# The output projection of a hybrid decoder block: the last four token blocks by seven half products a pair, the attention rows of its weights converted ahead, and three factor chains in place of seven

## The chip, the cores and the metric

The kernel runs on one core of one Trainium2 chip. The metric is the device time of one execution in microseconds (us), the median of several runs. The engines are TensorE (PE in the profile; PEld is its loading of the stationary operand), VectorE (DVE), ScalarE (ACT), GpSimd (POOL), and SyncE (SP), whose queue here issues every DMA.

## What is computed

One decoder block on x (1024 tokens by 1024 columns, float32):

```python
h = rmsnorm(x, norm1_w)
proj = h @ w_in                      # 1024 x 4104, split into heads, gates and decays
o_sb  = rmsnorm(stick_breaking_attention(q, k, v), sb_norm_w)  * silu(sb_z)    # 8 heads of 64
o_gdn = rmsnorm(gated_delta(gq, gk, gv, decay, beta), gdn_norm_w) * silu(g_z)  # 4 heads of 128
mixed = concatenate([o_sb, o_gdn])   # 1024 x 1024
out = rmsnorm(x + mixed @ w_out, final_norm_w)
```

The change concerns the last two lines, and the factors 1/sqrt(mean square) that scale the attention's output, head by head and token by token.

## The kernel before

**How products are made.** A float32 product is three passes of a faster format, called float32r in the code: each operand is split into a high part (h: a copy rounded by ScalarE) and a low part (l: the operand less h), and `mm3` (line 533) adds h·h, h·l and l·h into a PSUM bank of 128 x 512. A product of 128 tokens by 512 columns over 1024 rows is 8 x 3 = 24 matmuls; over 512 rows, a half product here, it is 12.

**How the order is set.** The program is not written in its final order. `block` (line 439) starts generators, such as projections, attention, the delta rule, and the output's parts, and a planner (`Model`, lines 138 to 311) decides: it keeps a list of ready instructions for VectorE, ScalarE, GpSimd and SyncE, sorted by a priority (`ck.prio`, the names on line 35; a lower number goes first), with estimated costs and delays (`cost`, `HOPS`). `interleave` (line 409) picks the generator that may issue TensorE work. What comes out is a fixed order on each engine. At run time each engine, and the SyncE queue, takes its instructions in that order, and one that waits holds up all behind it. Because each recorded operation goes through one helper, almost all instructions carry line 329 in the profile; they are told apart by tile names.

**The end of the program.** The projections run as filler down to the eight gate blocks z0 to z7 (line 30), each in two halves (".0" is the lower 512 tokens). Each half ends in a VectorE multiplication by `rbc` (zt<-pp,rbc), a sigmoid and a GpSimd product; the gates go to DRAM (gate_s), except that of z7. Then:

- `factors` (line 1470): for the four pairs of attention heads j, and for j = 3 for each quarter p of the tokens by itself, the mean squares (ss_s in DRAM) are loaded into `sst`, VectorE takes the root in ten steps on `rst` and `ust`, and the result is stored (rs_s). That makes seven chains.
- `out_weights` (line 1502): the eight row blocks of w_out are loaded (wor), scaled by the norm weights and split into woh and wol. Rows 4 to 7 (delta) come early; rows 0 to 3 (attention) are split when the projections are over, since their tiles take the memory of the projections' operand x (xh, xl). Only then is `fnw`, the final norm's weight, loaded.
- `mixed_delta` (line 1531) and `mixed_attention` (line 1545): for a token block b of 128, the delta rule's output (mx) and its gates (gt), and the attention's output (oa), its factors (rb) and its gates (ga) are loaded. VectorE scales mx by rsg; GpSimd multiplies rb by the gates.
- `prepare` (line 1562): the delta half is transposed on TensorE (pz<-step,mx) and multiplied by the gates, the attention half is oa times rb (mf), and both are split into mh and ml, the low part by GpSimd.
- `product` (line 1594): for each block, 16 pairs of a 512-column half and a row block, each three matmuls: 48 a block. Blocks 0 and 1 take their delta halves (rows 4 to 7) first, because these are ready before the attention's. VectorE adds the residual (y), ScalarE sums squares, VectorE takes the root (`_rsqrt1`, tiles sy and ry), scales, and SyncE stores the block. The last block's upper half goes in two pieces of 256 columns, so that its end is short.

The few lines that carry the product before:

```python
for n, k in [(n, k) for n in range(len(parts)) for k in ks]:
    if k < 4 and b == 0:
        yield wts[k][2]
    hs = parts[n]
...
    mm3(pt, mh[:, k, :], ml[:, k, :], wts[k][0][:, hs], wts[k][1][:, hs], k == 4, k == 3)
```

Of the kernel before, what the change touches and what calls it, by code (L numbers as in the profile page):

```python
# [10 lines left out]
F32 = mybir.dt.float32  # L11
# [6 lines left out]
P = 128  # L18
T = 1024
# [15 lines left out]
OUT_WEIGHTS, DELTA, WEIGHTS, COMBINED, LATE, BANK, SPLIT, RSTD, WINDOW, OUTPUT, RESULT, DECAYS = -1, 0, 2, 3, 0.5, 5, 4, -0.5, 10, 12, 20, 25  # L35
# [358 lines left out]

class Stream:
# [43 lines left out]
def block(tc, xT_d, x_d, n1_d, wE_d, wC_d, conv_d, alog_d, dtb_d, mixw_d, wo_d, fnw_d, out_d):  # L439
# [4 lines left out]
    with ExitStack() as top:  # L444
# [31 lines left out]
        sst, rst, ust = [cst.tile([P, 16], F32, name=n) for n in ("sst", "rst", "ust")]  # L476
# [24 lines left out]
        px = open_pool("px", ctx=proj_ctx, side="right")  # L501
        xh = px.tile([P, NK, T], F32R, name="xh")
        xl = px.tile([P, NK, T], F32R, name="xl")
# [70 lines left out]
        for k in korder:  # L574
# [228 lines left out]
        def z_evac(i):  # L803
            n = (i + 4) % NK

            def evac(pt, half):
                hs = slice(half * 512, (half + 1) * 512)
                zt = pr.tile([P, 512], F32, tag="kt", bufs=2, name="zt")
# [479 lines left out]
        def gdn_chain(h, g):  # L1288
# [6 lines left out]
            for j in range(4):  # L1295
# [29 lines left out]
                def out(c=c, j=j, s_in=s_prev, vr=vr):  # L1325
# [4 lines left out]
                    oe = gi[0].tile([P, P], F32, tag="goe", name="goe")  # L1330
# [139 lines left out]
        def factors():  # L1470
            for j, p in [(0, 3), (1, 3), (2, 3)] + [(3, p) for p in range(4)]:
                yield from until(f"t{j}{p}")
                m = 16 if j < 3 else 4
                ss, rs, us = [t[:, 0:m] for t in (sst, rst, ust)]
                src, dst = [(d[j] if j < 3 else d[j, p]).rearrange("p h t -> (p h t)" if j < 3 else "h t -> (h t)").rearrange("(q f) -> q f", f=m) for d in (ss_s, rs_s)]
                yield S.dma_start(ss, src)
                _rsqrt(V, None, rs, ss, m, us)
                r = S.dma_start(dst, rs)
                for b in range(NB) if j < 3 else (2 * p, 2 * p + 1):
                    flags[f"c{j}{b}."] = r  # L1480
                yield


        wts = {}
        pools = {}

        def wo_raw(k):
            pool, tag, bufs = {4: (pools[0], "wor", 1), 5: (pools[0], "xr", 1), 6: (pools[0], "mh", 1), 7: (pools[0], "ml", 1),  # L1490
                               0: (at_, "v2a", 2), 1: (at_, "kh", 1), 2: (at_, "sg7", 1), 3: (at_, "v2a", 2)}[k]
            r = pool.tile([P, D], F32, tag=tag, bufs=bufs, name="wor")
            wts[k] = r
            return S.dma_start(r, wo_d[k * P:(k + 1) * P, :])

        def wo_split(k):
            w, pool = wts[k], pools[k < 4]
            wh, wl = [pool.tile([P, D], F32R, name=f"wo{n}{k}") for n in "hl"]
            A.activation(wh, w, AF.Copy, scale=mixw[:, k:k + 1])
            wts[k] = (wh, wl, V.scalar_tensor_tensor(wl, w, mixw[:, k:k + 1], wh.bitcast(F32), ALU.mult, ALU.subtract))  # L1500

        def out_weights():
            yield lambda: "g" in flags
            gdn_ctx.close()
            pools[0] = open_pool("f0", before=gd.ops() + gi[0].ops())
            flags["pool0"] = True
            raws = [wo_raw(k) for k in range(4, NK)]
            for k in range(4, NK):
                yield raws[k - 4]
                wo_split(k)  # L1510
            flags["wo"] = True
            yield lambda: f"s{SBH - 1}{NB - 1}" in flags
            for k in (0, 1):
                wo_raw(k)
            flags["late"] = True
            yield lambda: f"e{SBH - 1}{NB // 2 - 1}" in flags
            for k in (2, 3):
                wo_raw(k)
            yield lambda: "proj" in flags
            proj_ctx.close()  # L1520
            pools[1] = open_pool("f1", before=px.ops(), side="right")
            for k in range(4):
                ck.prio = LATE if k else OUT_WEIGHTS
                wo_split(k)
            fnw = wts["fnw"] = pools[1].tile([P, D], F32, name="fnw")
            S.dma_start(fnw, fnw_d.partition_broadcast(P))
            flags["fnw"] = True

        ready = {}

        def mixed_delta():
            for b in range(NB):
                yield lambda: "wo" in flags and "rsg" in flags and "z3" in flags and (b < 2 or "late" in flags and f"e{SBH - 1}{NB // 2 - 1}" in flags) and (b < 3 or "fnw" in flags and f"m{b - 3}" in flags)
                fi = pools[0]
                mx = fi.tile([P, 512], F32, **(dict(tag="wor") if b % 3 == 2 else dict(tag="mx", bufs=2, turn=True)), name="mx")
                gt = (at_.tile([P, 4, P], F32, tag="sg4", name="gt") if b % 3 == 2 else fi.tile([P, 4, P], F32, tag="gt", bufs=2, turn=True, name="gt"))
                S.dma_start(mx, og_s[b].rearrange("p h d -> p (h d)"))
                S.dma_start(gt, gate_s[4:8, :, b * P:(b + 1) * P].rearrange("k e t -> e k t"))
# [4 lines left out]
                flags[f"mx{b}1"] = r  # L1543

        def mixed_attention():
            for b in range(NB):
                bs = slice(b * P, (b + 1) * P)
                yield lambda: all(f"c{j}{b}." in flags for j in range(4)) and "z6" in flags and (b < 2 or f"l{b - 2}" in flags)
                oa, rb, ga = [pools[0].tile([P, n, P], F32, tag=t, bufs=2, turn=True, name=t) for t, n in (("oa", 4), ("rb", 4), ("ga", 3))]
                S.dma_start(oa, o_s[:, :, bs].rearrange("j r t -> r j t"))  # L1550
                for u in range(2):
                    S.dma_start(rb[64 * u:64 * u + 64], rs_s[:, b // 2, u, (b % 2) * P:(b % 2) * P + P].unsqueeze(0).to_broadcast([SBD, 4, P]))
                S.dma_start(ga, gate_s[0:3, :, bs].rearrange("k e t -> e k t"))
                G.tensor_tensor(rb[:, 0:3, :], rb[:, 0:3, :], ga, ALU.mult)
                yield lambda: ("z7" if b >= 4 else "z7.0") in flags
                ready["oa", b] = (oa, rb)
                flags[f"oa{b}0"] = G.tensor_tensor(rb[:, 3, :], rb[:, 3, :], gate7[b // 4][:, (b % 4) * P:(b % 4) * P + P], ALU.mult)

        def halves():
            return [(0, 1), (1, 1), (0, 0), (1, 0)] + [(b, g) for b in range(2, NB) for g in (1, 0)]  # L1560

        def prepare():
            for b, g in halves():
                bs = slice(b * P, (b + 1) * P)
                if g:
                    yield from until(f"mx{b}1")
                    mx, gt = ready["mx", b]
                    yield lambda: b == 0 or "late" in flags and (b < 2 or f"f{b - 2}" in flags)
                    pool = (pools[0], at_)[b % 2]
# [122 lines left out]
```

## Time and profile before

| | us |
|---|---|
| median of 3 runs | 665.47 (664.96 to 666.32) |
| the profiled execution | 666.25 |
| its span, first to last instruction | 664.5 |
| TensorE busy in the span | 647.4 |
| VectorE busy | 529.6 |
| ScalarE busy | 404.1 |
| GpSimd busy | 314.1 |
| mean granted TensorE clock | 0.995 |

The profile is one execution. The time of the profiled execution is 1.75 us longer than its span. In rows of a timeline the first number is the start from the span's beginning, the second the length, both in us; `out<-in` are tile names with their numbers left out, and the bracket at the end is the idle time before the instruction and what ended it. In group rows the count stands behind x, then busy us, mean ns of one, and the idle time before them. In rows of windows the engines follow as TensorE, weight loads, VectorE, ScalarE, GpSimd, then the granted clock, the DMA engines' share and GB/s.

### The profile page before, as it was taken

To read this page: it belongs to the slowest core of one execution; us is meant where nothing else is said; L and a number is where in the kernel's file an instruction comes from. 1 tells how busy PE (TensorE), PEld (TensorE's weight loads), DVE (VectorE), ACT (ScalarE), POOL (GpSimd) and SP (SyncE) were. 2 spreads that over 40 slices of the span, in tenths; PEclk is the share of its full clock that TensorE was granted. 3 is DMA by queue.
4 is the path that set the end of the run, shared out by engine and by line. 5 is a ranking of instruction groups with operands and counts; after the bars stand their busy time and mean duration, and the time that the engine had idled before them with its cause. 6 is when DMAs were issued, how large, how long until landed. Compare 5 with 4: busy or idle time off the path is not lost.

```text
span 664.5 us, 11883 instructions
## 1 busy us (share of the span) xinstructions
PE 647.4 (97%) x3950; PEld 550.8 (83%) x3950; DVE 529.6 (80%) x1122; ACT 404.1 (61%) x1028; POOL 314.1 (47%) x285
## 2 busy tenths in 40 slices
PE   8999999999999999999999999999999999899995
PEld 8998888888778888788888888888888888687884
DVE  6998789776998779887787889887878973779643
ACT  7975675544796758865868775577858642122121
POOL 0000212059952689536894238983354652632511
PEclk9999999999999999999999999999999999899999
DMA  8846852487061462217254226343165657567421
GB/s 314 324 159 206 280 192 95 161 259 236 24 187 45 143 232 70 61 48 239 73 171 119 69 62 203 115 128 120 24 208 184 224 163 223 142 220 203 149 78 63
DMA packets 81965, 103.22 MB, mean 155 GB/s; under 512 B 17808, under 2 KB 51696, under 8 KB 81904
## 3 DMA queue, kind: packets, MB, share of 16 engines
q1 hardware_dynamic: 81904, 102.47, 48.4%
q8 instruction: 31, 0.51, 0.3%
q14 instruction: 30, 0.25, 0.1%
HBM read 74.55 MB, written 27.89 MB: 154 GB/s over the span
## 4 chain that ended last, share of the span: by engine, by line
PE 69%; DVE 8%; ACT 8%; DMA 6%; POOL 4%; issue 2%; SPq 2%; POOLq 0%; ACTq 0%; DVEq 0%
PE pp L329 37%; PE pz L329 22%; PE po L329 6%; PE pc L329 4%; SPq L329 2%; DVE cc L329 2%; DMA r<-xT 2%; ACT pz L329 2%; POOL tm L329 2%; ACT xr L329 1%; DMA ga<-gate_s 1%; DMA kl<-qk_s 1%; DMA qk_s<-kt 1%; DVE wol L329 1%; DVE pp L329 1%
## 5 line engine op out<-in xcount | busy, mean ns | idle before, releaser
L329 PE MATMUL pp<-xh,weh 128*128 128x512 f32 x336 | 141.0, 420 | 0.6 <-DVE pre L329 0.6
L329 PE MATMUL pp<-xh,wel 128*128 128x512 f32 x336 | 132.1, 393 | 0.5 <-POOL wel L329 0.5
L329 PE MATMUL pp<-xl,weh 128*128 128x512 f32 x336 | 131.4, 391 | 0.0
L329 POOL TENSOR_TENSOR sg<-sg,cc 128x128 f32<-128x128 f32 (+3 forms) x64 | 77.2, 1210 | 57.8 <-DVE cc L329 40.2
L329 POOL TENSOR_TENSOR wel<-wer,weh 128x512 fp32r<-128x512 f32 x40 | 52.6, 1314 | 54.5 <-ACT weh L329 54.4
L329 PEld LDWEIGHTS pp<-xh,wel 128*128 128x128 f32 x336 | 63.1, 188 | 15.4 <-POOL wel L329 0.9
L329 PEld LDWEIGHTS pp<-xh,weh 128*128 128x128 f32 x336 | 63.3, 188 | 10.4 <-DVE pre L329 1.5
L329 PEld LDWEIGHTS pp<-xl,weh 128*128 128x128 f32 x336 | 63.5, 189 | 8.7
L329 POOL TENSOR_TENSOR tm<-xs,br 128x32 f32<-128x32 f32 (+7 forms) x64 | 59.8, 935 | 7.3 <-DVE xs L329 5.4
L329 ACT ACTIVATE ah<-pz 128x512 fp32r<-128x512 f32 (+1 forms) x80 | 43.7, 561 | 31.4 <-PE pz L329 30.1
L329 ACT ACTIVATE sg<-pz,sel 128x384 f32<-128x384 f32 (+3 forms) x96 | 54.1, 591 | 11.4 <-PE pz L329 10.5
L329 DVE TENSOR_TENSOR_SCAN cc<-pz,step 128x384 f32<-128x384 f32 (+2 forms) x64 | 53.6, 846 | 5.9 <-ACT pz L329 3.8
L329 DVE TENSOR_TENSOR al<-pz,ah 128x512 fp32r<-128x512 f32 (+1 forms) x80 | 49.5, 627 | 9.8 <-ACT ah L329 9.4
L329 ACT ACTIVATE pz<-pz,sel 128x384 f32<-128x384 f32 (+3 forms) x96 | 53.6, 568 | 0.1
L329 ACT ACTIVATE xr<-y 128x1024 f32<-128x1024 f32 (+2 forms) x10 | 8.9, 890 | 71.6 <-DVE y L329 52.7
L329 PE MATMUL pz<-step,sg 128*128 128x128 f32 x288 | 44.5, 275 | 0.6 <-DVE cc L329 0.6
L329 PE MATMUL po<-ah,v2a 128*128 128x256 f32 (+1 forms) x160 | 42.8, 292 | 0.0
L329 POOL TENSOR_TENSOR kq<-kq,pre 128x512 f32<-128x512 f32 x16 | 20.9, 1307 | 43.5 <-ACT kq L329 39.0
L329 PE MATMUL pp<-woh,mh 128*128 128x512 f32 (+1 forms) x104 | 39.6, 381 | 0.5 <-DVE rst L329 0.5
L329 DVE TENSOR_TENSOR_SCAN cc<-pz,cc,step 128x512 f32<-128x512 f32 (+1 forms) x32 | 38.7, 1209 | 1.8 <-DVE cc L329 0.5
L329 PE MATMUL po<-al,v2a 128*128 128x256 f32 (+1 forms) x160 | 39.2, 281 | 0.0
L329 PE MATMUL pp<-wol,mh 128*128 128x512 f32 (+1 forms) x104 | 39.2, 377 | 0.0
(310 smaller groups left out, 1770.9 us busy)
## 6 DMA issues: line engine op xcount, KB each, us to landing
wer<-wE SPq DMA_DIRECT2D x40, 256.0 KB
xr<-x SPq DMA_DIRECT2D x16, 512.0 KB
r<-xT SPq DMA_DIRECT2D x8, 512.0 KB
v_s<-v2e SPq DMA_DIRECT2D x16, 256.0 KB
qk_s<-sqh SPq DMA_DIRECT2D x16, 256.0 KB
qk_s<-kt SPq DMA_DIRECT2D x16, 256.0 KB
q<-qk_s SPq DMA_DIRECT2D x8, 512.0 KB
v2a<-v_s SPq DMA_DIRECT2D x8, 512.0 KB
```

The source lines that it names most:

```text
L329: ins = f(*args, **kw).ins
```

## The change

**Seven half products a pair.** Token blocks 4 to 7 are taken as two pairs. With a11 and a12 for the delta and attention halves of the pair's first block, a21 and a22 for those of the second, and the weights as four quadrants (11 and 12: the delta rows, lower and upper columns; 21 and 22: the attention rows), the four outputs of a pair come from seven half products of 512 rows, in the manner of Strassen and Winograd, in place of eight. The seven take sums of the operands (su, s3) and of the weights (T1 to T4). These sums are made by VectorE and GpSimd, and all are split again into high and low parts: mo and mp for the operands, wt1h to wt4l for the weights. The outputs are put together from the PSUM banks by additions into the residual (xr, wc). Blocks 0 to 3 keep their 48 matmuls.

**Weights.** The delta rows are split into wdh and wdl as before. The attention rows are loaded while attention still runs, scaled in place by ScalarE, and split into pieces (wa) that lie in the attention's own tiles, so they need not wait for the memory of x. The rows for the sums are loaded a second time where their buffer has been given up: 14 loads of 512 KB in place of 8. A pool of six row buffers (raw) holds weight rows and residual rows by turns. xh and xl become two tiles each, one for each half of the tokens, so that the lower half's memory is free when z7.0 is done; for that three conversions of 1024 columns at the start of the program become two of 512 each. `fnw` is loaded into `rbc`.

**Factors.** Chains: one for heads j = 0 to 2 (48 columns wide), one for j = 3 and quarters 0 to 2, one for j = 3 and the last quarter. In `prepare` the splits' low parts move from GpSimd to VectorE; in `mixed_delta` the scaling of mx moves from VectorE to ScalarE. The loads of the attention halves have a generator of their own, `load_attention`, and those of the residual too, `residual`.

The diff, cut to its core:

```diff
+OUT_WEIGHTS, DELTA, WEIGHTS, COMBINED, LATE, BANK, SPLIT, RSTD, WINDOW, OUTPUT, RESULT, DECAYS, SUMS, SCALES, PIECES = -1, 0, 2, 3, 0.5, 5, 4, -0.5, 10, 12, 20, 25, 22, 21, 11
...
-            for hs in () if k > 3 else (slice(0, T),) if k else (slice(0, 256), slice(256, 512), upper):
+            for hs in () if k > 3 else (lower, upper) if k else (slice(0, 256), slice(256, 512), upper):
...
         def factors():
-            for j, p in [(0, 3), (1, 3), (2, 3)] + [(3, p) for p in range(4)]:
-                yield from until(f"t{j}{p}")
-                m = 16 if j < 3 else 4
+            for heads, sums, quarters in ((slice(0, 3), "23", range(4)), (3, "32", range(3)), (3, "33", range(3, 4))):
+                yield from until(f"t{sums}")
+                m = 48 if sums == "23" else 4 * len(quarters)
...
         def out_weights():
...
+            def pieces(k, tags):
+                h, l = [at_.tile([P, D], F32R, tag=tag, bufs=bufs, name="wa") for tag, bufs in tags]
+                w = wa[(2, 3, 0, 1).index(k)]
+                ck.prio = PIECES
+                A.activation(h, w, AF.Copy)
+                r = V.tensor_tensor(l, w, f32(h), ALU.subtract)
...
+            def sums(w, u):
+                ck.prio = SUMS
+                (b11, b12), (b21, b22) = half(w), half(u)
+                for d, a, b, op in ((b11, b12, b11, ALU.subtract), (b12, b12, b22, ALU.subtract), (b22, b11, b22, ALU.subtract), (b21, b21, b22, ALU.add)):
+                    V.tensor_tensor(d, a, b, op)
+                return {"T2": b22, "T1": b11, "T3": b12, "T4": b21}
...
+            for k in range(2, 4):
+                pair = []
+                for n in (4 + k, k):
+                    yield lambda: f0.room("raw", 6)
+                    pair.append(row(n))
...
-                    r = V.tensor_scalar(mx[:, gs], mx[:, gs], rsg[:, g, b:b + 1], None, ALU.mult)
+                    r = A.activation(mx[:, gs], mx[:, gs], AF.Copy, scale=rsg[:, g, b:b + 1])
...
+        def split(i, src, eng):
+            h, l = slot(i)
+            A.activation(h, src, AF.Copy)
+            ready[i] = eng.tensor_tensor(l, src, f32(h), ALU.subtract)
...
-                ready[b, g] = G.tensor_tensor(lv, fv, hv.bitcast(F32), ALU.subtract)
...
+                G.tensor_tensor(su, a21, a22, ALU.add)
+                V.tensor_tensor(s3, a21, a11, ALU.subtract)
...
+                V.tensor_tensor(su, a11, su, ALU.subtract)
...
+                G.tensor_tensor(su, a12, su, ALU.add)
...
+                plan = {"A": (0, "11"), "B": (1, "21"), "C": (5, "T2"), "D": (4, "T1"), "E": (2, "T3"), "F": (3, "T4"), "G": (6, "22")}
...
+                for q in "ADCFEBG" if last else "ABCDEFG":
+                    i, wname = plan[q]
+                    tag, bufs = {"A": (("pc", "po")[p % 2], 1), "D": ("pz", 4), "G": ("pz", 4)}.get(q, ("pp", 2))
...
+                    if q == "A":
+                        w = pr.tile([P, 512], F32, tag="wer", bufs=2, name="wc")
+                        add(ya[:, 0], pt)
+                        A.activation(w, pt, AF.Copy)
+                    elif q == "B":
+                        add(ya[:, 0], pt)
+                    elif q == "C":
+                        add(w, pt)
+                        add(ya[:, 1], w, G)
+                    elif q == "D":
+                        add(yb[:, 1], pt)
+                        add(ya[:, 1], pt)
+                    elif q == "E":
+                        add(w, pt)
+                        add(yb[:, 0], w, G)
+                        add(yb[:, 1], w, V if last else G)
+                    elif q == "F":
+                        add(yb[:, 0], pt)
+                    else:
+                        add(ya[:, 1], pt)
```

The planner turns this into new orders. The first place is VectorE at the last projection half (zt is its evacuation), before: rst, ust and sst are the factor chain, mf the attention halves of blocks 0 and 1, wol the low parts of the attention rows, y the first addition of an output.

```order
L329 TENSOR_TENSOR zt<-pp,rbc 128x512
L329 TENSOR_TENSOR ust<-ust,sst 128x4
L329 TENSOR_TENSOR mf<-oa,rb 128x512
L329 SCALAR_TENSOR_TENSOR wol_7225<-wor,sel,woh_7224 128x1024
L329 SCALAR_TENSOR_TENSOR wol_7229<-wor,sel,woh_7228 128x1024
L329 SCALAR_TENSOR_TENSOR wol_7233<-wor,sel,woh_7232 128x1024
L329 SCALAR_TENSOR_TENSOR wol_7237<-wor,sel,woh_7236 128x1024
L329 SCALAR_TENSOR_TENSOR rst<-ust,rst 128x4
```

The same place now: oa is block 0's attention half, mo its low part, wt3l and wt4l are low parts of the weight sums, and pz<-pz,gt is the delta half of block 2.

```order
L329 TENSOR_TENSOR oa<-oa,rb 128x512
L329 SCALAR_TENSOR_TENSOR rst<-ust,rst 128x4
L329 TENSOR_TENSOR zt<-pp,rbc 128x512
L329 SCALAR_TENSOR_TENSOR ust<-rst 128x4
L329 TENSOR_TENSOR wt3l<-wor,wt3h 128x512
L329 TENSOR_TENSOR mo<-oa,mo 128x512
L329 TENSOR_TENSOR pz<-pz,gt 128x512
L329 TENSOR_TENSOR ust<-ust,sst 128x4
```

The four operations of 1024 columns are gone from here; the attention half stands ahead of the last evacuation, and operations on the weights' sums stand among the others.

The second place is the SyncE queue where the residual rows of blocks 2 and 3 (xr<-x) are loaded, before: mx, gt, oa, rb and ga belong to blocks 3 to 5, and out<-y is a finished block.

```order
L329 DMA oa<-o_s 128x4x128
L329 DMA xr<-x 128x1024
L329 DMA rb<-rs_s 64x4x128 x2
L329 DMA xr<-x 128x1024
L329 DMA ga<-gate_s 128x3x128
L329 DMA mx<-og_s 128x512
L329 DMA out<-y 128x1024
```

Now, with the loads of block 5 first:

```order
L329 DMA rb<-rs_s 64x4x128 x2
L329 DMA oa<-o_s 128x4x128
L329 DMA ga<-gate_s 128x2x128
L329 DMA ga<-gate_s 128x128
L329 DMA xr<-x 128x1024
L329 DMA out<-xr 128x1024
L329 DMA xr<-x 128x1024 x2
L329 DMA out<-xr 128x1024
```

The residual rows of block 2 have moved behind the attention loads of block 5, and those of the later blocks stand close together, between the first stores.

More of the change, by code (lines that the diff above doesn't have):

```diff
@@ L1485, in block @@
+        wmat, wready = {}, {}
+        f32 = lambda ap: ap.bitcast(F32)
         pools = {}
[L1489 to L1500, printed above, removed]
+        last_window, last_pair = f"s{SBH - 1}{NB - 1}", f"e{SBH - 1}{NB // 2 - 1}"
+        two = lambda ap: ap.rearrange("p (c n) -> p c n", c=2)
+        def quadrant(name, hi, lo, part=None):
+            for k in range(4) if part is None else part:
+                wmat[name, k] = (hi[:, k, :], lo[:, k, :])
@@ new lines, in half, with split_row @@
+            def half(w):
+                return w[:, lower], w[:, upper]
+            def split_row(w, h, l, prio):
+                ck.prio = prio
+                A.activation(h, w, AF.Copy)
+                return V.tensor_tensor(l, w, h.bitcast(F32), ALU.subtract)
+            for k in range(4):
+                w = f0.tile([P, D], F32, tag="raw", bufs=6, turn=True, name="wor")
+                raws.append((w, S.dma_start(w, wo_d[(4 + k) * P:(5 + k) * P, :])))
+            for k, (w, r) in enumerate(raws):
+                yield r
+                sc = mixw[:, 4 + k:5 + k]
+                A.activation(wdh[:, k], w, AF.Copy, scale=sc)
+                wready["11", k] = wready["12", k] = V.scalar_tensor_tensor(wdl[:, k], w, sc, f32(wdh)[:, k], ALU.mult, ALU.subtract)
@@ L1519, in out_weights @@
+            for name in ("T2", "T1"):
+                for k in range(2):
+                    split_sums(*todo[k], name)
             yield lambda: "proj" in flags
             proj_ctx.close()
[L1521 to L1526, printed above, removed]
@@ new lines, in out_weights, with use, free, slot @@
+            flags["ts"] = True
+        def use(b, g):
+            if b < 2:
+                return 2 * (1 - g) + b
+            return 2 * b + 1 - g
+        def free(i):
+            return i % 7 < len(slots) and (i < 7 or i - 7 in done)
+        def slot(i):
+            return slots[i % 7]
+        def residual():
+            for b in range(NB):
+                yield lambda: ("w0" if b < 2 else "ts") in flags and "t33" in flags and pools[0].room("raw", 6)
+                x = pools[0].tile([P, D], F32, tag="raw", bufs=6, name="xr")
+                ck.hold(True, x)
+                S.dma_start(x, x_d[b * P:(b + 1) * P, :])
+                ready["x", b] = two(x)
+                xraw[b] = x
@@ L1531, in mixed_delta @@
         def mixed_delta():
             for b in range(NB):
[L1533 to L1536, printed above, removed]
+                yield lambda: "wo" in flags and "rsg" in flags and "z3" in flags and pools[0].room("gt", 2) and (b < 2 or "t33" in flags) and (b < 2 or f"m{b - 2}" in flags)
```

369 lines of the change are left out of this document (255 added, 114 removed).

## The prediction

> **What bounds the kernel now.** I read the page first, then the chain of waits, then the end of the program by windows, and there the engines' own timelines. The page's busy line and its row of the granted TensorE clock (40 slices) come first:
>
> ```profile
> span 664.5 us, 11883 instructions
> PE 647.4 (97%) x3950; PEld 550.8 (83%) x3950; DVE 529.6 (80%) x1122; ACT 404.1 (61%) x1028; POOL 314.1 (47%) x285
> PEclk9999999999999999999999999999999999899999
> ```
>
> TensorE is busy 97% of the span. That figure is modelled, so the chain has to bear it out. These are its last parts (start, length, engine, tile):
>
> ```profile
> 557.52 7.98 DMA ga<-gate_s
> 565.57 1.03 POOL rb L329
> 566.62 1.76 DVE mf L329
> 568.38 7.63 DVE wol L329 x4
> 576.05 1.22 PE po L329 x2
> ...
> 611.48 11.16 PE pp L329 x48
> 623.07 11.16 PE pp L329 x48
> 634.67 19.59 PE pp L329 x96
> ```
>
> The reader is to see two things. From 577 us on the chain is TensorE alone, 48 products of 512 columns a token block, 11.16 / 48 = 0.2325 us each. Just before, it runs through the gate load, GpSimd, and four VectorE conversions of the attention rows of the output weights (wol). The windows (TensorE busy, weight loads, VectorE, ScalarE, GpSimd, clock, DMA share) show what that turn costs:
>
> ```profile
> 560.00:580.00 20.00, 18.23 (x71) 14.17 (x70) 14.66 (x25) 5.95 (x7) 11.37 (x9) 0.91 0.64 169
> 580.00:600.00 20.00, 19.50 (x91) 15.76 (x90) 13.96 (x40) 4.61 (x8) 6.52 (x6) 1.00 0.66 201
> 600.00:620.00 20.00, 20.00 (x90) 16.18 (x89) 16.99 (x41) 4.39 (x8) 9.14 (x8) 1.00 0.77 229
> 620.00:640.00 20.00, 20.00 (x92) 16.23 (x91) 12.72 (x27) 4.39 (x8) 6.51 (x6) 1.00 0.25 85
> 640.00:664.50 24.50, 17.09 (x98) 14.67 (x96) 9.17 (x27) 3.62 (x9) 2.74 (x3) 0.94 0.16 64
> ```
>
> Only 560 to 580 has both idle TensorE time and a low clock, 0.91. The TensorE timeline names them:
>
> ```profile
> 560.45 0.39 PE L329 MATMUL po<-woh,mh 128*128 128x512 f32 x1
> ...
> 574.10 0.50 PE L329 MATMUL po<-wol,mh 128*128 128x512 f32 x1 [0.80 <-DVE wol L329]
> ...
> 576.05 0.80 PE L329 MATMUL po<-wol,mh 128*128 128x512 f32 x1 [0.97 <-DVE wol L329]
> ...
> 579.55 0.39 PE L329 MATMUL pc<-woh,mh 128*128 128x512 f32 x1
> ...
> 599.62 0.47 PE L329 MATMUL pp<-woh,mh 128*128 128x512 f32 x1 [0.49 <-DVE rst L329]
> ...
> 656.81 0.28 PE L329 MATMUL pp<-woh,ml 128*128 128x256 f32 x1
> ```
>
> So the output product runs from 560.45 to 657.1 us, with two waits of 0.80 and 0.97 us on the conversions, and one of 0.49 us on a factor chain (rst). Behind the first two, the eight products from 576.05 to 579.55 take 3.50 us where eight at 0.2325 take 1.86: 1.64 us lost to a low clock.
>
> **The change, part by part.** The sum is made against the profiled execution: 666.25 us, its span of 664.5 and 1.75 around it. It lies 0.78 above the median of the three runs shown, 665.47, to which the differences are applied in the end.
>
> *Half products.* Four blocks by 48 products are 192; two pairs by seven half products of 4 x 3 are 168. The 24 removed lie on a TensorE that runs back to back: 24 x 0.2325 = **-5.58 us**. [...]
>
> *Attention rows converted ahead.* The four wol conversions leave the turn. After the last projection's evacuation (zt), VectorE has short work there, and the weights' pieces have long been split. The 0.80 + 0.97 and the 1.64 behind them go: **-3.41 us**. What is late next is the attention operand of block 0. Its chain now is gate, rb, oa, mo, and TensorE first has 48 products of the delta halves (11.2 us) after 560.45, so the chain may end at 571 to 572. It ended in its mf step at 568.4 before for block 1, so I leave about 3 us of cover, and more for block 0. [...]
>
> *Three factor chains.* VectorE's waits are these, with the four conversions behind them:
>
> ```profile
> 560.18 0.17 DVE L329 TENSOR_SCALAR rst<-sst 128x4 int32<-128x4 int32 x1 [4.23 <-DMA sst<-ss_s]
> 566.62 1.76 DVE L329 TENSOR_TENSOR mf<-oa,rb 128x512 f32<-128x512 f32 x1 [4.23 <-POOL rb L329]
> 568.30 7.69 DVE L329 SCALAR_TENSOR_TENSOR wol<-wor,sel,woh 128x1024 fp32r<-128x1024 f32 x4
> ...
> 583.58 1.35 DVE L329 SCALAR_TENSOR_TENSOR sy<-ry,sy 128x1 f32<-128x1 f32 x1
> ...
> 603.16 0.67 DVE L329 TENSOR_TENSOR mf<-pz,gt 128x512 f32<-128x512 f32 x1
> 603.76 0.67 DVE L329 TENSOR_TENSOR mf<-oa,rb 128x512 f32<-128x512 f32 x1
> ...
> 608.12 0.22 DVE L329 SCALAR_TENSOR_TENSOR sy<-ry,sy 128x1 f32<-128x1 f32 x1
> ...
> 608.57 1.28 DVE L329 SCALAR_TENSOR_TENSOR y<-y,ry,fnw 128x1024 f32<-128x1024 f32 x1
> ```
>
> The 4.23 us for sst held up nothing on TensorE, which was in its last projection and then in the delta halves. Of the chains only the 0.49 at 599.62 reached TensorE: **-0.49 us**.
>
> *VectorE's new work.* Behind the last projection's evacuation the order of before has 28 VectorE operations of 512 columns, that of after 82: sums and splits of weights and of the pairs' operands, which were GpSimd's, and more additions. At 0.60 from start to start (603.16 to 603.76) that is 49 us; with six scalings at 1.28, some 76 tiny ones at about 0.15, and 2 for the rest, 70 us. TensorE's work there is 360 x 0.2325 = 83.7 us and eight sets of transposes, about 87. VectorE has room on average, but GpSimd holds it up. A tiny step takes 0.22 alone (608.12) and 1.35 beside GpSimd (583.58). Grouped over 560 to 664.5 us (count, busy, mean in ns):
>
> ```profile
> L329 DVE SCALAR_TENSOR_TENSOR sy<-ry,sy 128x1 f32<-128x1 f32 x24 | 10.7, 444 | 0.7
> L329 DVE SCALAR_TENSOR_TENSOR ry<-sy,ry 128x1 f32<-128x1 f32 x24 | 8.0, 331 | 0.7
> ```
>
> GpSimd's own groups there:
>
> ```profile
> L329 POOL TENSOR_TENSOR ml<-mf,mh 128x512 fp32r<-128x512 f32 x14 | 18.2, 1314 | 24.9 <-ACT mh L329 24.9
> L329 POOL TENSOR_TENSOR rb<-rb,ga 128x384 f32<-128x384 f32 x7 | 8.3, 1187 | 15.0 <-DMA rb<-rs_s 7.7 <-DMA out<-y 7.1
> ```
>
> The 24 sy steps take 10.7 us where 24 x 0.22 are 5.3, the ry steps 8.0 where 24 x 0.15 are 3.6: 9.8 us lost. With the wider kinds I estimate 14, on 36.3 us of GpSimd in the five windows (11.37 + 6.52 + 9.14 + 6.51 + 2.74): four tenths. GpSimd keeps its rb products and gets sums and additions of 1.31 us, about 30 us in all, so VectorE loses some 12 more: 82 of 87 us. That is tight. New TensorE waits cost between 0 and, if the same pair as before comes back, 3.41; I take the middle: **+1.7 us**. Below nothing they cannot be, as no wait but those named is left to remove. ScalarE takes the delta blocks' scalings (mx) and the weights' first halves in its free time; it is busy 5.95 of the first 20 us and less later.
>
> *The residual rows* come later: one SyncE load for block 2 is issued behind block 5's, when a weight buffer is free, and a bank must be drained within 24 products (5.6 us) of its end. This is within the 0 to 3.41 as well.
>
> *The last block.* Rows after TensorE's end, the last one SyncE's issue of the two result stores:
>
> ```profile
> 657.13 0.42 DVE L329 TENSOR_TENSOR y<-pp,xr 128x256 f32<-128x256 f32 x1 [1.68 <-PE pp L329]
> 657.59 0.42 ACT L329 ACTIVATE xr<-y 128x256 f32<-128x256 f32 x1 [2.33 <-DVE y L329]
> ...
> 660.08 0.72 ACT L329 ACTIVATE y<-y,ry 128x512 f32<-128x512 f32 x1 [1.99 <-issue]
> ...
> 660.83 0.81 SPq L329 DMA_DIRECT2D out<-y  x2
> ```
>
> From 657.1 to the end were 7.4 us. In the changed order the root of block 7 stands between the two halves of block 6's last product, with one 512-column multiplication and six tiny steps. Block 7's store of 512 KB goes out just ahead of the final two of 256 KB. Costs 0 (all ready in time) to 2.5 (multiplication behind a GpSimd one, 0.67 + 1.31, and half a microsecond of store): **+1.5 us**, nearer to the upper end, since block 7's squares end only about when they are needed.
>
> *The first stage.* Three conversions of 1024 columns become six of 512, in a stage where ScalarE has no free time:
>
> ```profile
> 8.56 0.62 ACT L329 ACTIVATE xh<-r 128x512 fp32r<-128x512 f32 x1
> 9.08 1.14 ACT L329 ACTIVATE xh<-r,sel 128x1024 fp32r<-128x1024 f32 x1
> ```
>
> 3 x (2 x 0.62 - 1.14) = **+0.3 us** at most. TensorE may start on a lower half earlier, so it is 0 to 0.3; I take the upper.
>
> Sum: -5.58 - 3.41 - 0.49 + 1.7 + 1.5 + 0.3 = -5.98. Profiled 660.3, from the median 665.47 - 5.98 = **659.5 us**.
>
> **The rivals.** *A, the turn still waits.* If the store and load of the longer factor chain or the gate load (7.98 us here) end after the delta halves, the -3.41 does not come: 659.5 + 3.4 = 662.9. For it: that load. Against it: 11.2 us of cover for block 0 and 17 for block 1.
>
> *B, nothing new waits.* Operands are ready early and the tail stays as it was: -5.58 - 3.41 - 0.49 + 0.3 = -9.18, 656.3. For it: four or five microseconds idle of VectorE a block in before (20 - 12.72 in a window of 1.7 blocks). Against it: the 82 of 87.
>
> *C, VectorE becomes the bound; slower.* If each microsecond of GpSimd shuts out VectorE, it has 70 + 30 = 100 us of work from about 561.5 on (the last projection ends at 560.45), and about 6 us of waits for TensorE's last products cannot be filled: it ends at 667.5, where the last scaling ended at 660.8 (660.08 + 0.72). The time is 665.47 + 6.7 = 672.2. It decides once VectorE is over 87 + 6 us, the lead that the pairs' operands have. For it: 1.35 against 0.22. Against it: only four tenths of GpSimd's time was lost to VectorE. [...]
>
> *D, both partly.* The turn waits as before (+3.4) and a second such pair of waits comes in the pairs (3.4 instead of 1.7): 664.6, no change.
>
> *E, the change does not do what it says.* VectorE may still wait for a factor, as before at 560.18; since that was covered, the time is the forecast's, and it needs no chance of its own.
>
> **How the numbers follow.** Forecast 0.50, A 0.18, B 0.17, D 0.06, C 0.09. About 0.2% (1.3 us) is what a measurement of this kernel can tell from no change. Faster: forecast, A and B, 0.85; within 0.2%: D, 0.06; slower: C, 0.09. The range runs from just under B, 655.5, to D, 664.5, and leaves out C and the odd end of the others.
>
> **What would show it.** In the changed profile: TensorE behind its last projection has 360 products of 512 columns (48 halves of them) at 0.2325; no wait on wol's successor (wa), and no clock under 1.00 there; no sst wait on VectorE over 1 us; VectorE busy over 80% from 560 us on; between TensorE's end and the end of the span 8 to 10 us, not 7.4. I am wrong if a stretch of low clock comes back at the first attention halves (A) or if TensorE waits for operands (mo, mp) or banks repeatedly (C).

## The result, and the profile after

| | before | after |
|---|---|---|
| median of 10 runs, us | 664.40 (662.81 to 666.32) | 673.01 (667.00 to 677.96) |
| ratio of after to before, without the run of 677.96 | | 1.0117, 95% interval 1.0082 to 1.0153 |
| the profiled execution, us | 666.25, span 664.5 | 671.28, span 669.6 |

The change made the kernel slower by 1.2%, where the forecast was 0.9% faster. An execution can hold one longer stretch of granted clock 0.50, as the profiles of four kernels below do (e2, e4, e6 and e10: 6.8 to 13.7 us long, ahead of the output product, which then starts at 566 to 570 us and not at 561 to 563), so a median also says how many of its executions held one.

The page of after, to be read against that of before:

```profile
span 669.6 us, 11905 instructions
PE 643.1 (96%) x3914; PEld 544.8 (81%) x3914; DVE 543.4 (81%) x1120; ACT 438.9 (66%) x1113; POOL 311.1 (46%) x283
PEclk9999999999999999999999999999999999988998
PE 58%; DMA 13%; DVE 11%; ACT 9%; POOL 3%; issue 3%; SPq 2%; DVEq 0%; ACTq 0%; POOLq 0%
```

TensorE has 36 instructions fewer (3950 to 3914): 24 products, and 12 more because the last half product, like the last block before, goes in pieces of 256 columns, of which there are now 24 and not 48. So the products did go. But the clock row has a dip in two slices near the end, and the chain that ended last is TensorE's for 58% of the span, 69% before, and DMA's for 13%, 6% before. The windows of the end say where:

```profile
560.00:580.00 20.00, 20.00 (x92) 16.29 (x91) 12.39 (x21) 7.16 (x14) 8.02 (x9) 1.00 0.68 189
580.00:600.00 20.00, 17.63 (x72) 13.62 (x71) 14.93 (x33) 13.15 (x29) 5.43 (x7) 0.91 0.78 218
600.00:620.00 20.00, 17.79 (x71) 13.96 (x70) 18.73 (x38) 7.31 (x15) 5.82 (x4) 0.91 0.65 228
620.00:640.00 20.00, 18.38 (x82) 14.40 (x81) 15.32 (x29) 6.09 (x14) 8.54 (x9) 1.00 0.44 126
```

The turn at 560 to 580, where before had its idle time and its low clock, is clean: 20.00 of 20 us at 1.00. The next three windows, all but clean before (19.50, 20.00 and 20.00), lack 1.6 to 2.4 us of TensorE each, and two run at 0.91. TensorE's timeline names the waits:

```profile
586.08 0.33 PE L329 MATMUL pz<-step,mx 128*128 128x128 f32 x1 [0.83 <-ACT mx L329]
587.47 0.62 PE L329 MATMUL pz<-step,mx 128*128 128x128 f32 x2 [1.05 <-ACT mx L329]
588.57 0.47 PE L329 MATMUL pz<-step,mx 128*128 128x128 f32 x1 [0.48 <-ACT mx L329]
588.70 2.91 PE L329 MATMUL pz<-wa,mo 128*128 128x512 f32 x6
591.41 0.47 PE L329 MATMUL pp<-wdh,mp 128*128 128x512 f32 x1
...
605.02 0.64 PE L329 MATMUL pp<-wdh,mp 128*128 128x512 f32 x1 [2.21 <-DVE xr L329]
...
608.45 0.72 PE L329 MATMUL pp<-wdh,mp 128*128 128x512 f32 x2
...
629.85 1.21 PE L329 MATMUL pz<-step,mx 128*128 128x128 f32 x4 [1.62 <-ACT mx L329]
...
659.34 1.69 PE L329 MATMUL pz<-wa,mo 128*128 128x256 f32 x12 [0.52 <-DVE xr L329]
```

I count as lost what lies between two starts beyond 0.2325 us for a product of 512 columns, 0.1175 for one of 256 and 0.11 for a transpose. Block 5's transposes, which wait three times for ScalarE's scaling of a row (mx), and the low clock behind them (the six products from 588.70 take 2.71 us, not 1.40) lose 4.46. The wait for block 2's bank at 605.02 and the low clock up to 608.45 lose 4.03. Block 7's transposes at 629.85 lose 2.40, the last half product 0.8: 11.7 us in all, where before lost 4.5, 3.8 in its two waits on wol with their low clock and 0.6 at the wait for rst and around it.

What holds the waiting engines up is in the chain of waits (start, length, what):

```profile
577.87 6.62 DMA ga<-gate_s
...
584.93 10.68 DMA ga<-gate_s
595.61 0.07 issue
595.68 1.02 POOL rb L329
596.70 0.02 issue
596.73 0.69 DVE oa L329
...
604.37 0.61 DVE xr L329
604.98 0.04 issue
605.02 9.99 PE pp L329 x35
...
622.05 7.33 DMA mx<-og_s
...
629.39 0.41 ACT mx L329
...
629.85 2.38 PE pz L329 x9
```

A gate row (ga) of 192 KB is 10.68 us on its way. GpSimd multiplies it into rb, and VectorE's next instruction in its order, the product oa times rb, stands and waits 3.59 us for that, with everything queued behind it. From 596.73 on VectorE works that queue off without a gap, and only at 604.29 comes to the addition that frees the bank. In VectorE's timeline:

```profile
596.73 0.69 DVE L329 TENSOR_TENSOR oa<-oa,rb 128x512 f32<-128x512 f32 x1 [3.59 <-POOL rb L329]
...
603.14 1.22 DVE L329 SCALAR_TENSOR_TENSOR ry<-sy,ry 128x1 f32<-128x1 f32 x1
604.29 0.68 DVE L329 TENSOR_TENSOR xr<-pp,xr 128x512 f32<-128x512 f32 x1
```

GpSimd lengthens the queue: it multiplies from 602.58 for 1.77 us, and the tiny step at 603.14 takes 1.22 us beside it, where the same step takes 0.15 with GpSimd idle. Two earlier tiny steps take 0.69 and 0.42 beside GpSimd, not 0.21 and 0.15. That is 1.8 us of the 7.6, and without it the wait of 2.21 would have been some 0.4 us (an estimate from these rows). The residual row itself was there: issued at 598.22, landed 3.7 us later, at 601.9. Block 7's mx is a plain late load, issued at 622.05 and 7.33 us on its way.

So the theory, **L**: the plan puts instructions that need a row too close behind the row's load. The planner reckons 1.1 us to a transfer's start and 1.5 us behind its end (`Model.start`); on the chip the three rows above take 6.6 to 10.7 us. For the gate row it reckons some 3.3 (1.1, 0.7 for its bytes by `cost`, and 1.5), and the trace has 10.68. The rival, **V**: VectorE, with ScalarE, has too much work (rival C of the prediction in a milder form). One sign of V is in after too: from 600 to 620 us VectorE is busy 18.73 of 20 us.

### The profile page after: what moved, and what is told of

It reads as the page before. It is cut to its first block, busy times and chain, and to the rows that moved or that the text cites. A ratio compares the mean times of both kernels' runs of the same rounds, so it can differ in the third digit from the quotient of the medians.

```text
span 669.6 us, 11905 instructions
## 1 busy us (share of the span) xinstructions
PE 643.1 (96%) x3914; PEld 544.8 (81%) x3914; DVE 543.4 (81%) x1120; ACT 438.9 (66%) x1113; POOL 311.1 (46%) x283
## 4 chain that ended last, share of the span: by engine, by line
PE 58%; DMA 13%; DVE 11%; ACT 9%; POOL 3%; issue 3%; SPq 2%; DVEq 0%; ACTq 0%; POOLq 0%
PE pp L329 30%; PE pz L329 20%; PE po L329 6%; DMA ga<-gate_s 4%; PE pc L329 3%; SPq L329 2%; ACT pz L329 2%; DMA r<-xT 2%; DMA gate_s<-zt 2%; POOL tm L329 2%; DMA xr<-x 1%; DMA wer<-wE 1%; ACT sg L329 1%; DMA mx<-og_s 1%; DVE al L329 1%
## 5 line engine op out<-in xcount | busy, mean ns | idle before, releaser
L329 PE MATMUL pz<-kh,q 128*128 128x384 f32 (+3 forms) x96 | 37.2, 394 | 0.6 <-DVE al L329 0.2
L329 DVE TENSOR_REDUCE xs<-tm 128x16 f32<-128x32 f32 (+7 forms) x64 | 27.3, 427 | 12.2 <-POOL tm L329 11.9
L329 PEld LDWEIGHTS pz<-step,sg 128*128 128x128 f32 x288 | 33.0, 141 | 4.2 <-issue 1.0
```

What stands on the lines that cost most here:

```text
L329: ins = f(*args, **kw).ins
```

## The experiments

Each kernel ran together with the kernel before. "Lost" is counted as above over the output product of the profiled execution, "first" is the start of its first product and "end" the end of its span.

| kernel | median, us | before, us | ratio (95% interval) | first, lost, end, us |
|---|---|---|---|---|
| changed kernel again (e0_again) | 673.71 | 667.38 | 1.0109 (1.0067 to 1.0151) | 563.30, 13.1, 671.5 |
| loads reckoned later (e1_lat) | 664.20 | 667.38 | 0.9983 (0.9952 to 1.0013) | 561.98, 4.9, 661.8 |
| residual row free to go ahead (e2_xr) | 667.54 | 667.38 | 1.0010 (0.9975 to 1.0045) | 566.60, 7.8, 669.5 |
| without half products (e3_plain) | 669.87 | 667.38 | 1.0051 (1.0017 to 1.0084) | 562.27, 5.5, 667.3 |
| idle products in the wait (e4_warm) | 671.66 | 664.93 | 1.0097 (1.0061 to 1.0132) | 567.47, 8.3, 673.4 |
| e1 and e2 together (e5_both) | 662.40 | 664.93 | 0.9976 (0.9942 to 1.0009) | 561.76, 3.3, 660.1 |
| e5, two sums by GpSimd (e6_lowG) | 661.64 | 664.93 | 0.9956 (0.9932 to 0.9980) | 565.98, 2.1, 663.1 |
| before, loads reckoned later (b1_lat) | 664.50 | 664.93 | 0.9993 (0.9963 to 1.0024) | 560.97, 2.4, 662.9 |
| e3, loads reckoned later (e7_plain_lat) | 664.20 | 663.73 | 1.0011 (0.9982 to 1.0041) | 561.82, 1.0, 662.3 |
| changed, two sums by GpSimd (e9_lowG) | 668.39 | 663.73 | 1.0078 (1.0043 to 1.0113) | 561.63, 10.1, 666.7 |
| e5, four sums by GpSimd (e10_allG) | 672.12 | 663.73 | 1.0106 (1.0064 to 1.0147) | 569.83, 10.5, 675.5 |
| before again (b0_again) | 664.88 | 663.95 | 1.0020 (0.9984 to 1.0055) | 561.68, 1.7, 662.9 |

**The changed kernel again.** No edit.

> The changed kernel once more, with nothing edited, for a second profile and for its spread. Theory L (late loads): TensorE waits in the output product for rows that come late through SyncE's queue (mx of blocks 5 and 7, the residual row of block 2), and each wait is followed by a stretch of low clock. Then a second execution shows the same waits at the same instructions, 4 to 6 us in all, with 4 to 7 us more in low clock behind them, and the time is 667 to 678. Theory V (a crowded engine: VectorE or ScalarE with the new sums, splits and scalings): the waits wander from product to product, and VectorE is busy over 90% between the waits.

The waits are again those for block 5's mx (1.06 and 0.48), block 2's bank (4.97) and block 7's mx (1.49). They are at fixed places, as L has it; only their lengths change. They make 8.0 us, more than the 4 to 6 expected. The wait of 4.97 stands behind a wait of 5.42 us of VectorE for rb.

**Loads reckoned later.** From the last gate block (z7) on:

```diff
-            self.at(self.dma + 1500, self.finish, op)
+            self.at(self.dma + (5500 if self.late else 1500), self.finish, op)
```

> The planner reckons that every load from the last projection on ends 4 us later than it did (5500 ns behind its transfer instead of 1500), which moves the transposes of blocks 2 to 7 later in TensorE's order and puts block 2's residual row four loads earlier in SyncE's. No work changes. Theory L: the waits on mx of blocks 5 and 7 go (4.5 and 2.4 us with their low clock in the profile of the changed kernel) and the one behind the residual row (4.0) goes in part: 673 - 7 to 11 = 662 to 666. Theory V: the work of VectorE and ScalarE is the same, so the time stays at 671 to 675.

664.2: the ratio falls from 1.0109 to 0.9983, about 8 us, with the same instructions in another order. The waits on mx are gone, and what VectorE waits for over the output product has changed. In after:

```profile
DVE oa L329 <- POOL rb L329: 11.1, 6, 3.6
DVE xr L329 <- PE pp L329: 4.2, 4, 1.8
DVE wc L329 <- PE pp L329: 2.9, 3, 2.1
```

With loads reckoned later (total, times, longest):

```profile
DVE xr L329 <- PE pp L329: 5.1, 4, 1.5
DVE xr L329 <- PE po L329: 3.2, 1, 3.2
DVE xr L329 <- PE pz L329: 2.9, 2, 2.1
```

VectorE no longer stands behind GpSimd's rows; it waits for TensorE's results, as it should. The gate rows still take 6.4 to 7.7 us, far more than the planner had reckoned; they are only not waited for. V is out as the cause of most of the loss. One long wait is left, on a bank again:

```profile
599.69 0.50 PE L329 MATMUL pp<-wdh,mp 128*128 128x512 f32 x1 [2.25 <-DVE xr L329]
```

There VectorE has had no gap for 19 us, from 579.40 on, with sums and splits of weight rows among its operations, so this wait is V's.

**The residual row free to go ahead.**

```diff
-                yield lambda: ("w0" if b < 2 else "ts") in flags and ...
+                yield lambda: ("w0" if b < 3 else "ts") in flags and ...
```

> Block 2's residual row may be loaded as soon as a raw buffer is free; it no longer waits until all eight weight rows of the sums are loaded and split. Theory L: the wait of 2.2 us on block 2's bank and the low clock behind it go, 4.0 us in all; the waits on mx stay: 673 - 4 = 669. In theory V the bank is late because VectorE is late, not the row: no difference, 671 to 675. A third outcome is that the two weight rows behind it come later and TensorE waits for the sums (wt) instead.

The wait for block 2's bank is gone, and by the ratios the gain is 1.0%, 6.6 us, more than the 4 expected. But the row was not what the bank waited for in after; it had landed 2.4 us earlier. So the gain came by another way than the expected one. With the row planned early, VectorE's order is another: its longest wait for rb near there is 0.92 us, and the bank is free in time. Block 5's transposes still wait, 3.25 us here.

**The change without half products.** `plain` lists all eight blocks, and the sums and the second load of four weight rows are left out:

```diff
-            return [(0, 1), (1, 1), (0, 0), (1, 0), (2, 1), (2, 0), (3, 1), (3, 0)]
+            return [(0, 1), (1, 1), (0, 0), (1, 0)] + [(b, g) for b in range(2, NB) for g in (1, 0)]
-                t = sums(*wd[k])
-                split_sums(k, t, "T2", "T1", "T3", "T4")
```

> The change without its half products: all eight blocks by 48 products, attention rows converted ahead, three factor chains; the sums of weights and operands and the second load of four weight rows are gone. It has 24 products more than the changed kernel (5.6 us). Theory L: without the four row loads and the wait for the sums the residual rows come early, and the waits of the tail go, so 673 + 5.6 - 8 to -11.6 = 667 to 670 with the mx waits that may stay, or, from the kernel before, 664.4 - 3.4 - 0.5 + 0 to 2.4 = 660.5 to 663 if all waits go. If the half products are innocent and something else in the change costs the time (scalings on ScalarE, the new conversions at the start), it is 673 + 5.6 = 678.

The time, 669.87, is within what L gave. By the ratios it is 0.6% below the changed kernel's, with 24 products more, though the intervals overlap a little. Waits of 1.23 on mx and 0.73 and 1.60 on banks stay, so the tight plan is not the half products' alone: scaling on ScalarE and two buffers for mx and gt in place of three are in this kernel too. They were not tried by themselves.

**Idle products in the wait.**

```diff
+                        if (b, n) == (3, 0):
+                            yield lambda: ps.room("pz", 4)
+                            tp, wh = pz(), wmat["11", 0][0]
+                            for _ in range(12):
+                                TE.matmul(tp, wh[:, 0:P], wh, start=True, stop=True)
```

> The changed kernel with 12 idle products of 512 columns (2.8 us, their result is overwritten) ahead of the first product of block 3, where TensorE waits 2.2 and 5.0 us for block 2's bank in the two profiles of the changed kernel. Nothing else is edited. If a low clock follows because TensorE stood idle, the wait shrinks to 2.2 us or less, and the stretch of 12 to 14 products at 0.43 us behind it (1.7 and 2.2 us lost) is gone or shorter; the 12 products cost nothing as far as they lie in the wait: 673 - 2 to + 1. If the low clock has nothing to do with the wait, the stretch stays and the time is 673 to 675.

The wait is 1.86, and the products behind it run at full clock:

```profile
606.34 2.91 PE L329 MATMUL pz<-wdh 128*128 128x512 f32 x12
611.11 0.50 PE L329 MATMUL pp<-wdh,mp 128*128 128x512 f32 x1 [1.86 <-DVE xr L329]
611.44 0.40 PE L329 MATMUL pp<-wdl,mp 128*128 128x512 f32 x1
611.67 0.63 PE L329 MATMUL pp<-wdh,mp 128*128 128x512 f32 x2
```

That is what idling as the cause asks for, but waits of 1.60 and 2.21 us in other kernels (e3, b1) were not followed by low clock either, so this profile alone does not settle it. The last section sets idle time and clock side by side. The time did not gain what the expectation hoped: the ratio, 1.0097, is that of the changed kernel.

**Both edits together.** The two diffs above.

> Loads reckoned 4 us later and block 2's residual row free to go ahead of the weight rows, together. Theory L in its plain form: the one long wait that is left with loads reckoned later (2.25 us behind block 2's bank and 1.7 of low clock) goes too: 664.2 - 4 = 660. Theory V as it stands now: with the loads on time VectorE is the next limit, since it runs without a gap from 587 to 601 us there, and the bank waits for VectorE's backlog and not for the row; then the wait only moves and the time stays at 663 to 665.

662.4, between the two. No wait over 0.8 us is left, the clock row is 9 in all slices but the last, and 3.3 us are lost. VectorE is now full where the weight sums fall:

```profile
580.00:600.00 20.00, 20.00 (x94) 16.30 (x93) 19.11 (x43) 12.04 (x28) 7.05 (x8) 1.00 0.81 251
600.00:620.00 20.00, 20.00 (x89) 16.19 (x89) 19.72 (x41) 7.69 (x16) 5.88 (x6) 1.00 0.63 185
```

That is 38.8 of 40 us: with the loads on time, V's engine is the next to be late, at banks and operands (0.62 for mp, 0.72 for xr).

**Two sums' low parts by GpSimd**, on top of both:

```diff
-            LOWS = {"T1": V, "T2": V, "T3": V, "T4": V}
+            LOWS = {"T1": V, "T2": V, "T3": G, "T4": G}
```

> As the one before, with the low parts of two of the four weight sums (wt3l, wt4l: eight operations of 512 columns, 4.8 us of VectorE) made by GpSimd instead of VectorE. Theory V: VectorE's backlog shrinks by 4.8 us and any wait for a bank left in the kernel before goes: 1 to 3 us faster than that one. If loads alone decide, or if GpSimd holds VectorE up by as much as it takes off, no difference or up to 2 us slower.

Lost time falls to 2.1 us. The median is 0.8 us below e5's, within the intervals. It is the one version whose whole interval lies below the kernel before: 0.9956, 0.9932 to 0.9980.

**The kernel before with loads reckoned later.** The same line in its planner.

> The kernel before with the same later reckoning of loads from the last projection on; a control. TensorE's order is the one of the kernel before. If late loads are a matter of the changed output product, the time is that of the kernel before within 1.5 us and TensorE's waits behind 560 us stay those on wol (0.80, 0.97) and rst (0.49). If any plan of this kernel gains by the reckoning, it is 3 us or more faster, and the gain of the changed kernel by it isn't a repair of the change.

No difference, 0.9993. So the reckoning repairs something of the change; it isn't a gain that any plan of this kernel has. The waits on wol were not there in its profile; one of 2.21 for a bank was.

**Without half products, loads reckoned later.**

> The change without its half products (all eight blocks by 48 products), with loads reckoned 4 us later from the last projection on. It stands to the changed kernel with loads reckoned later as the plain kernel does to the changed one, and prices the 24 products where loads come on time. If they are worth their 5.6 us there, this kernel takes 664.2 + 5.6 = 670 less what VectorE's lighter work gives back; if the plain kernel loses its waits of 1.23, 0.73 and 1.60 us as well it takes 666 to 667, and the half products are worth 2 to 5 us. If it takes 664 or less, the half products bring nothing even then.

The number, 664.2, is not to be set beside the 664.2 of e1: the kernel before, run together with each, took 663.7 here and 667.4 there. By the ratios, 1.0011 and 0.9983, the half products are worth 0.3%, 1.9 us, and against e5 and e6, which have further edits, 0.35% and 0.55%, 2.3 and 3.7 us: the lower part of the 2 to 5 expected. The intervals of e1 and e5 overlap this kernel's, so the times alone do not show it; the profiles do. The plain kernel is all but free of waits, 1.0 us lost. Its profile and e5's begin the output product at the same time, 561.82 and 561.76, and so price the half products where loads come on time (in one execution of each): -5.58 for 24 products, +2.3 for VectorE's waits (3.3 lost, not 1.0), +1.0 for the end (651.66 to 660.1 is 8.4 us, 654.89 to 662.3 is 7.4), which makes -2.3; the spans give -2.2.

**VectorE's relief alone, loads as they were.** The LOWS line, on the changed kernel.

> The changed kernel with the low parts of two of the four weight sums (wt3l, wt4l) made by GpSimd, and nothing else: the relief of VectorE by 4.8 us without any change to the loads. If VectorE's work were what holds TensorE up (theory V), it is 3 to 5 us faster: 668 to 670. If late loads are (theory L), the waits on mx and behind block 2's residual row stay, and the time is 671 to 675.

The number, 668.39, is what V expected, but the kernel before, run together with it, was quicker as well; the ratio, 1.0078, is 0.3%, 2 us, below the changed kernel's, and the intervals overlap. So the time speaks for neither. The profile is part L's and part V's:

```profile
588.74 1.21 PE L329 MATMUL pz<-step,mx 128*128 128x128 f32 x4 [1.23 <-ACT mx L329]
603.39 0.80 PE L329 MATMUL pp<-wdh,mp 128*128 128x512 f32 x1 [4.37 <-DVE xr L329]
```

A wait on block 5's mx is there, as L has it; block 7's is gone. The wait at block 2's bank stays and is no shorter, but here no long wait for rb stands close ahead of it. VectorE waits 2.02 us for rb at 588.31, then is busy 10.46 of the 10.66 us up to the addition at 602.66, and its last step, a scaling, takes 2.29 us beside GpSimd:

```profile
600.44 2.29 DVE L329 SCALAR_TENSOR_TENSOR xr<-xr,ry,rbc 128x1024 f32<-128x1024 f32 x1
```

That is V's backlog, with GpSimd in it, and no wait for the residual row shows. So at this bank late rows are not the whole cause. Relief of VectorE by GpSimd alone gains at most a part.

**All four sums' low parts by GpSimd**, on e5.

> Loads reckoned later, block 2's residual row free to go ahead, and the low parts of all four weight sums made by GpSimd (16 operations of 512 columns, 9.6 us of VectorE, some 21 us of GpSimd). With two sums moved the time was 661.6. If VectorE is what is left, 1 to 2 us less: 660. If GpSimd now makes the rows of the attention halves (rb) late, or shuts VectorE out for as long as it helps, 662 to 666.

A miss on the far side, by the second of the two reasons given. TensorE waits 4.49 us for an operand (mp), whose source, the product oa times rb, VectorE reaches only at 599.53, without one idle stretch behind 587.84:

```profile
590.68 1.14 DVE L329 SCALAR_TENSOR_TENSOR sy<-ry,sy 128x1 f32<-128x1 f32 x1
...
592.35 1.25 DVE L329 SCALAR_TENSOR_TENSOR ry<-sy,ry 128x1 f32<-128x1 f32 x1
...
596.13 1.19 DVE L329 SCALAR_TENSOR_TENSOR ry<-sy,ry 128x1 f32<-128x1 f32 x1
597.36 2.25 DVE L329 SCALAR_TENSOR_TENSOR xr<-xr,ry,rbc 128x1024 f32<-128x1024 f32 x1
```

Steps of 0.15 to 0.21 us take over 1.1, the scaling of a block 2.25 where it takes 1.27 alone: from 590 to 600 us GpSimd is busy 8.01 us and VectorE 9.89, with 15 operations; in e5 it makes 24 between 582 and 592, where GpSimd is busy 2.03. That is rival C's mechanism, and here it decides.

**The kernel before again.** No edit.

> The kernel before with nothing edited, for a second profile of it. Its profiled execution of 666.25 us was the slowest but one of its first ten runs (662.81 to 666.32). If the two waits on wol and the low clock behind them (3.41 us) belong to every execution, they stand here at the same two instructions and the time is 664 to 666.3. If that execution was unlucky, the waits are shorter or no low clock follows them, less than 2 us is lost there, and the time is 662.8 to 664; then the 3.41 us of the forecast was too large a saving against the median by what is missing here.

```profile
574.73 0.50 PE L329 MATMUL po<-wol,mh 128*128 128x512 f32 x1 [0.18 <-DVE wol L329]
...
576.67 0.49 PE L329 MATMUL po<-wol,mh 128*128 128x512 f32 x1 [0.97 <-DVE wol L329]
577.00 0.40 PE L329 MATMUL po<-woh,ml 128*128 128x512 f32 x1
577.24 0.39 PE L329 MATMUL pc<-woh,mh 128*128 128x512 f32 x1
```

The waits are 0.18 and 0.97, with full clock behind them (0.235 from start to start), and there is no wait for rst. What is lost there is 1.7 us, counted from start to start, where the execution shown before lost 3.8, and the 0.49 is nothing. That execution, 1.85 us above the median of its ten runs, was an unlucky one.

## Why the prediction was wrong

The step that failed is "New TensorE waits cost between 0 and, if the same pair as before comes back, 3.41; I take the middle: +1.7 us", with "This is within the 0 to 3.41 as well" for the residual rows. The new waits and the low clock behind them were 11.7 us in the one profile and 13.1 in the other. I had bounded them by the wait that the change removes, which says nothing of the waits that a new plan can make. The rows for it were quoted: 4.23 us of VectorE for rb, 4.23 for sst, 7.98 us for a gate load. I asked whether VectorE had time enough on average, 82 of 87 us, and not whether each row would be there when the engine's order came to it. In after VectorE is busy 78.5 of the last 107.6 us, so the 82 of work were about right, and waits 11.1 us for rb.

The other steps:

- *Half products, -5.58*: they went, and at full clock TensorE's rate stayed near 0.2325 (in after, the 12 products from 640.56 us take 2.81). Right.
- *Attention rows ahead, -3.41*: no wait is left at the turn, and its window is full at 1.00, so rival A did not happen. As a saving it was mis-sized against the median, as far as a second profile tells: that one loses 1.7 there, and nothing by the factor chain's 0.49, so of -3.90 some -1.7 was left.
- *The last block, +1.5*: TensorE ended at 661.0, the span 8.5 us later, against 7.4 before: +1.1. Right; of the 2.5 at the upper end, the half microsecond of store was my estimate, and no run shows it by itself.
- *The first stage, +0.3*: the first projection product starts at 58.5 and 58.8 us in the two profiles of the changed kernel, at 57.3 before, and at 57.3 to 57.7 in e1, e2, e3 and e5, whose start is instruction for instruction the same. So 0 to 1.5, where 0.3 was to be the most; why the two are later is open.
- *Rival C* named VectorE as the bound at 672.2. The time came within a microsecond of that, by another mechanism. VectorE was a quarter idle, and with its work unchanged and loads reckoned later the loss was gone. It became the next limit in e1 and e5. What the rival describes, GpSimd shutting VectorE out, cost 1.8 us of VectorE ahead of block 2's bank in after, and decided only in e10.
- *What would show it*: I had said that I was wrong if TensorE waited repeatedly for operands or banks. It did, for mx and banks. I had also asked for VectorE busy over 80% from 560 us on; it was 73%.

The account of the two profiles shown: -5.6 for the products, -4.5 for before's lost time, +11.7 for after's, +2.4 for the first output product (562.85, 560.45 before), +1.1 for the end make +5.1, and the spans differ by as much. Of the 2.4 about 1.2 is the start; the second profile of before begins its output at 561.68, as e1, e5 and e7 do within 0.3, so the rest lies in the spread of one execution.

## What to carry to other kernels

Where each engine takes its work in a written order, a load's price is not its bytes (in after a row of 192 KB took 10.68 us and one of 256 KB 7.33) but the gap that the order leaves behind its issue: before a plan is made tighter, set the plan's reckoning of a load beside the loads' landing times in the trace. VectorE's busy share of 73% was no cover, because its queue stood 3.6 us for one row and gave the loss on to all that was behind it. And a saving is best read from two executions: one low clock stretch made the removed wait look twice the size (3.8 us) that it had in another execution (1.7).

## What the runs showed of the hardware

Low clock came after short idling. In the output product, six of seven waits of TensorE of 2.2 us or more (2.21 in after, 4.97 in e0, 2.25 in e1, 3.25 in e2, 4.37 in e9, 4.49 in e10) were followed by a stretch of products at 0.43 us, 1.7 to 2.8 us of loss; one of 2.21, in b1, was not. Of the shorter ones, alone or in groups, before's 0.80 + 0.97 and after's 0.83 + 1.05 + 0.48 were, and nearly the same groups in the second profiles (0.18 + 0.97 in b0; 1.06 + 0.48 in e0) were not.

The granted clock of before and after shows when. In before it goes to 0.50 at 576.01 us, for 3.41 us, and at 661.34, behind the last product; in after at 588.17 and at 605.24, for 3.41 us each, and at 663.26, behind the last product. In each of the two these starts lie a whole number of 3.413 us apart: 25 in before (85.33 us), 5 and 17 in after (17.07 and 58.02 us). So each output product can be cut into windows of that length, and the idle time of a window set beside the clock of the next. First two windows of before, then two of b1, of the same length:

```profile
572.60:576.01 3.41, 1.68 (x7) 0.72 (x5) 3.41 (x3) 0.00 (x0) 3.41 (x3) 1.00 0.52 125
576.01:579.42 3.41, 3.37 (x8) 2.73 (x9) 2.89 (x11) 0.00 (x0) 1.76 (x3) 0.50 0.17 45
593.04:596.45 3.41, 2.77 (x14) 2.03 (x13) 1.97 (x5) 0.00 (x0) 1.24 (x2) 1.00 0.76 247
596.45:599.86 3.41, 1.84 (x8) 1.56 (x9) 3.36 (x6) 1.87 (x4) 1.29 (x1) 1.00 0.64 198
```

In before TensorE stands 1.73 us of the first window, by its two waits of 0.80 and 0.97 together, and the next is at 0.50. In after it stands 1.97 us of the window ahead of 588.17 and 2.21 us of the one ahead of 605.24. The other windows of these two output products have 0.91 us of idle time or less, and behind none of them is the clock at 0.50; that holds for after's window from 588.17 too, itself at 0.50, with 0.40 us. In b1 a wait of 2.21, as long as after's, lies 0.64 us in one window and 1.57 in the next, the products behind it start 0.22 to 0.24 us apart, and the clock stays at 1.00. Between 1.57 and 1.97 us both were seen: behind before's 1.73 the clock is low, behind e4's wait of 1.86 the products are at full rate.

Low clock can last longer. In e0 and e9 the 12 products behind the waits of 4.97 and 4.37 us take 5.29 us, where 12 at 0.2325 take 2.79, and in e10 the mean clock from 600 to 610 us is 0.66, an estimated 6.8 us at 0.50. The long stretches ahead of the output product do not fit: e4's, from about 196 to 210 us, has a wait of 0.70 us ahead of it, at 193.37, and e6's, from about 468 to 478.5, one of 0.53, at 467.70. Their cause is open.
